# A decode step rebuilt: VectorE's state update replaced by ScalarE products and an adding transfer

## The chip, the cores and the metric

The kernel runs on 1 core of one Trainium2 chip. The metric is device time in microseconds (us): 2167.06 us for the kernel before, the median of 3 runs (2167.03 to 2169.21). Engines are called PE (TensorE), DVE (VectorE), ACT (ScalarE), POOL (GpSimd) and SP (SyncE). Each works through its own instructions in a fixed order and waits on the others by semaphores; SP and POOL also issue the transfers between HBM (the device's memory) and SBUF (the core's memory).

## The reference, cut to what matters

Two layers of a decoder trunk work on 512 prompt tokens and on 8 sample tokens with the same weights. Only the retention of the sample tokens is touched. Per layer, head h (4 of them) and sample b (8 of them) there is a 256 x 256 state S; with one new token the reference comes down to

```python
def retention_chunk(S, q, k, v, log_gamma):      # here L = 1
    scores = einsum('blhd,bmhd->bhlm', q, k) * decay          # decay = 1
    intra = einsum('bhlm,bmhe->blhe', scores, v)              # (q.k) v
    inter = einsum('blhd,bhde->blhe', q, S) * q_dec           # gamma_h (q S)
    S_new = exp(log_gamma * L) * S + einsum('blhd,blhe->bhde', k * k_dec, v)
    return S_new, intra + inter                  # S_new = gamma S + k v,  o = q S_new
```

with gamma_h = 1 - 2^(-5-h). S_new is an output; o goes through a group norm, a gate, and with the other heads into the product with W_out. Everything else of a layer (RMS norm, product with W_in, short convolution, prompt retention, product with W_out, the gate W_pg) is the same in both kernels.

## The kernel before

All tokens stand together as 520 columns. Each of the four big products (W_in's heads, W_in's convolution part, W_out, W_pg) goes through pairs of 128-row output tiles. A pair is done by one level of Strassen's scheme (`strassen`) or directly (`plain`), on fp32 operands split into a high and a low part: three matmuls per weight tile (`mm3`, lines 247 to 249). SP loads weights into a ring of raw tiles (line 312), DVE forms Strassen's sums in place (line 319), ACT writes the high part (line 229) and DVE the low part (line 230) into a second ring, the ring of splits. `SPLIT = 60` blocks of 128 columns are its size; an instruction that fills a part of it has to wait until PE is through with what stood there. Everything else lies in `NSLOT = 75` slots of 520 columns (operands, results, states).

The order on each engine is set at build time by a scheduler, which plans with priorities and with times of its own; `keep(...)` pins an instruction behind the one that was traced before it on its engine. Weight splits have a raised priority.

The decode step is a side line. `head` and the convolution loop call `sample()` about once or twice per pair: some calls lie in the middle of a pair (list `middle`, which `strassen` empties after its fifth product), some at its end. A call first does the step whose operands were loaded by the call before, then issues the next loads. There are 32 steps in a layer, 64 in all; a step is one (h, b):

- `sample_load` (lines 770 and 771): two transfers from POOL's queue: the state (256 KB, transposed so that the 128 partitions hold e, in two halves of 256 columns d) and k, q of this token broadcast to all partitions.
- `sample_step`: ACT scales the state by gamma (line 776), two DVE instructions add k times v (line 780, v is a number per partition in `vs`), POOL issues the store of the new state (line 781), and two DVE instructions form the dot products with q (line 784, result in `osum`).

After the last step of a layer, at the eighth convolution tile (j = 7), `sample_norm` makes the group norm of all 32 results (lines 1371 to 1389, `rsn` on POOL at line 1383) and writes the gated values `gs`. W_out's operands are built from 16 tiles; eight of them are `retained` tiles, each of which takes its last 8 columns from `gs` (line 1064) before it is split (lines 551 and 552). "Joint" below means the stretch from the last convolution pair to the first pairs of W_out.

Of the kernel before, what the change touches and what calls it, by code (L numbers as in the profile page):

```python
# [7 lines left out]
F32 = mybir.dt.float32  # L8
F32R = mybir.dt.float32r
AF = mybir.ActivationFunctionType  # L10
ALU = mybir.AluOpType
MUL, ADD, SUB = ALU.mult, ALU.add, ALU.subtract

P = 128
# [3 lines left out]
SEQ = 512  # L18
NS = 8
T = SEQ + NS  # L20
# [4 lines left out]
H = 4  # L25
# [1 line left out]
PLE = 256  # L27
PAST = 4096
EPS = 1e-6
NSLOT = 75  # L30
CH = 4
CHS = 4
CHA = 4
# [16 lines left out]
EARLY = 6  # L50


HEADS = [[0, 0, 0, 8] + [14] * 12, [0] + [14] * 15]
CONVS = [[14] * 2 + [16] * 13 + [14]] * 2
OUT_ROWS = [[0, 8, 16, 16, 16, 16, 16, 0]] * 2
# [6 lines left out]
RAW = 32  # L62
WARM = 8
FIRST = 8
SPLIT = 60


def F(ap):
# [11 lines left out]
class Slots:  # L80
# [8 lines left out]
    def get(self, dtype=F32):  # L89
        i = self.free.pop(0)  # L90
        self.count += 1
        t = self.pool.tile([P, T], dtype, tag=f"s{i}", name=f"slot{i}_{self.count}")
        self.used[id(t)] = (t, i)
        return t
# [97 lines left out]
def trunk_kernel(  # L192
# [6 lines left out]
    V, S, G, PE, DMA = nc.vector, nc.scalar, nc.gpsimd, nc.tensor, nc.sync  # L199
    SIDE = nc.gpsimd  # L200

    const = ctx.enter_context(tc.tile_pool(name="const", bufs=1))
# [7 lines left out]
    get, getr, put = slots.get, slots.getr, slots.put  # L210
# [6 lines left out]
    keep = tc.keep_in_program_order  # L217
# [340 lines left out]
        return op  # L558


    vec = const.tile([P, 160], F32, name="vec")

    def norm_g(l, k):
        return vec[:, 16 * l + k : 16 * l + k + 1]
# [11 lines left out]
    def kd(h, m):  # L576
        c = 112 + 4 * h + m
        return vec[:, c : c + 1]

    def gam(h):  # L580
        return vec[:, 128 + h : 129 + h]

    ident = const.tile([P, P], F32, name="ident")
    ones = const.tile([P, P], F32, name="ones")
# [4 lines left out]
    vs = const.tile([P, H, 2, NS], F32, name="vs")  # L589
    osum = const.tile([P, 2, H, NS], F32, name="osum")  # L590
# [84 lines left out]
    for a, b in ((0, 1), (1, 4), (4, 8), (8, 12), (12, 16)):  # L675
        raws = []
        if b == 1:
            raw = raw_ring.get(4)
            DMA.dma_start(raw.rearrange("p (m n) -> p m n", n=P), wi[0, 0:4, :, :P].rearrange("m p n -> p m n"))
            S.dma_start(vec, vecs)  # L680
            x = get()
            for n in (LEFT, RIGHT):
                DMA.dma_start(x[:, n], xT[0, :, n])
            xs.append(x)
            w = split_w(raw)
            ws = [[t[:, P * m : P * m + P] for t in w] for m in range(4)]
        else:
            for i in range(4):
                raws.append(load(wi[0, i, :, P * a : P * b]))
                if i < b - a:  # L690
                    x = get()
                    DMA.dma_start(x, xT[a + i])
                    xs.append(x)
            ws = [split_w(raw) for raw in raws]
            raw_ring.put(*raws)
        for k in range(a, b):
            X.ops[k] = split(xs[k], norm_g(0, k), free_src=False, halves=k % 2 == 0 and k < max(X.rows))
            for m in range(4):
                for h, n in enumerate((LEFT, RIGHT)):
                    product(first[m][h], ws[m], k - a, at(X.ops, [k], n), k == 0, k == KT - 1)  # L700
        if b == 1:
            raw_ring.put(raw)
            split_ring.put(*w)
            DMA.dma_start(ident, ident_d)
        else:
            for w in ws:
                split_ring.put(*w)
# [8 lines left out]
    for l in range(DEPTH):  # L716
# [24 lines left out]
        root, rb, rc, rs = prepare()  # L741
# [24 lines left out]
            return g  # L766

        def sample_load(h, b):
            st, kb = get(), get()
            SIDE.dma_start(st[:, :512], sret[l, h, b])  # L770
            SIDE.dma_start(kb[:, :512], kq[l, h, b].rearrange("c d -> (c d)").partition_broadcast(P))  # L771
            return h, b, st, kb

        def sample_step(h, b, st, kb):

            keep(S.activation(st[:, :512], st[:, :512], AF.Identity, scale=gam(h)))  # L776
            k = kb[:, 256:512]
            for e in range(2):
                c = slice(256 * e, 256 * e + 256)
                keep(V.scalar_tensor_tensor(st[:, c], k, vs[:, h, e, b : b + 1], st[:, c], MUL, ADD))  # L780
            SIDE.dma_start(o_rets[l, h, b], st[:, :512])  # L781
            for e in range(2):
                c = slice(256 * e, 256 * e + 256)
                V.tensor_tensor_reduce(k, st[:, c], kb[:, :256], 1.0, 0.0, MUL, ADD, osum[:, e, h, b : b + 1])
            put(st, kb)

        loaded = []

        def sample():

            if loaded:
                sample_step(*loaded.pop(0))
            if todo:
                loaded.append(sample_load(*todo.pop(0)))

        todo = []
# [20 lines left out]
        def retain(h):  # L817
# [28 lines left out]
            vf = []  # L846
            for e, z in enumerate(head(mt + 4)):
                t = z.slot if z.ps is None else copied(z.ps).slot
                V.scalar_tensor_tensor(vs[:, h, e, :], t[:, SEQ:T], 1.0 / 16, rb[:, SEQ:T], MUL, MUL)
                vf.append(t)  # L850
            aside_copy(h, 4, vf)
            todo.extend((h, b) for b in range(NS))
# [224 lines left out]
        for j in range(CJ):  # L1077
# [12 lines left out]
            t = get()  # L1090
# [8 lines left out]
            if j < CJ - 1:  # L1099
                middle.append(sample)  # L1100
            if j == CJ - 1:
                while loaded or todo:
                    sample()
                O.ready = 7
                sample_norm(nc, small, pr, osum, onesd, half_neg, gs, lambda k: gn_g(l, k))
# [45 lines left out]
        for k in range(2):  # L1151
            t = get()
# [326 lines left out]
```

## Time and profile before

| what | value |
|---|---|
| runs | 2169.21, 2167.03, 2167.06 us |
| profiled execution, span from the first to the last instruction | 2167.3 us (the page has no other time for it) |
| mean granted TensorE clock | 0.999 |
| PE busy | 2147.8 us, 17861 matmuls |
| DVE busy | 1896.1 us |
| ACT busy | 1264.5 us |
| POOL busy | 430.6 us |
| DMA, mean over the span | 179 GB/s |

In the profile a row `L780 DVE SCALAR_TENSOR_TENSOR slot<-slot,vs,slot 128x256 ... x128 | 56.1, 481 | 4.5 <-ACT slot L776 4.3` is a group: line, engine, operation, result and operands by the program's names, shape, count; then busy us and mean ns of one; then idle time of the engine just before these instructions and who ended it. The busy us are a union, so that instructions which overlap at their ends give less than count times mean. In a list of waits, `A <- B: total, times, longest` says that A's engine stood idle until B was done. The view of stretches gives the busy time of every engine in each.

### The profile page before, as it was taken

The page shows a single profiled execution, that of the slowest core. Times are in us where ns is not written, and L with a number is a line of the kernel's source. Part 1 is how long each engine was busy: PE and PEld are TensorE (multiplying, and loading weights), DVE is VectorE, ACT ScalarE, POOL GpSimd, SP SyncE. Part 2 cuts the span into 40 slices and gives each one's busy share as a digit, 9 for nine tenths or more (in the row PEclk, how much of TensorE's full clock was granted, in tenths as well). Part 3 has the DMA queues.
Part 4 walks back from the last instruction along what each step waited for, and adds up shares of the span by engine and source line. Part 5 has one row for each costly group of instructions (what it writes and reads, how often), then busy time and mean ns, then how long its engine had stood idle before and what let it go on. Part 6 is the DMA issues. An engine that isn't in the chain of part 4 may idle for free. (4 is left out here: it accounts for less than half of the span.)

```text
span 2167.3 us, 48178 instructions
## 1 busy us (share of the span) xinstructions
PE 2147.8 (99%) x17861; PEld 2142.1 (99%) x17861; DVE 1896.1 (87%) x3849; ACT 1264.5 (58%) x2647; POOL 430.6 (20%) x746
## 2 busy tenths in 40 slices
PE   9999999999999999999999999999999999999998
PEld 9999999999999999999999999999999999999998
DVE  8889988998999987987997988989999998879884
ACT  8656655565555655655765655565645555456565
POOL 2313222211001211200212222231111022011011
PEclk9999999999999999999999999999999999999999
DMA  8555565545543745645645566664464355566455
GB/s 288 171 175 197 181 217 184 178 157 175 158 129 118 238 156 187 215 154 160 215 144 175 172 213 191 189 209 170 151 182 149 120 158 202 176 207 200 128 164 198
DMA packets 182861, 387.31 MB, mean 179 GB/s; under 512 B 25888, under 2 KB 56352, under 8 KB 182624
## 3 DMA queue, kind: packets, MB, share of 16 engines
q1 hardware_dynamic: 128704, 212.98, 31.6%
q0 software_dynamic: 53056, 169.84, 23.8%
q8 instruction: 140, 2.29, 0.4%
q10 hardware_dynamic: 864, 1.39, 0.2%
q14 instruction: 97, 0.79, 0.1%
HBM read 318.96 MB, written 65.15 MB: 177 GB/s over the span
## 5 line engine op out<-in xcount | busy, mean ns | idle before, releaser
L247 PE MATMUL ps_g<-slot,split 128*128 128x260 f32 x5465 | 1531.6, 284 | 7.2 <-ACT slot L307 2.9
L248 PE MATMUL ps_g<-slot,split 128*128 128x260 f32 x5465 | 1534.3, 282 | 0.3 <-DVE slot L555 0.3
L249 PE MATMUL ps_g<-slot,split 128*128 128x260 f32 x5461 | 1519.9, 283 | 0.5 <-DVE split L230 0.5
L229 ACT ACTIVATE split<-raw 128x512 fp32r<-128x512 f32 (+2 forms) x1347 | 777.3, 596 | 583.1 <-DVE raw L319 213.2
L247 PEld LDWEIGHTS ps_g<-slot,split 128*128 128x128 f32 x5465 | 1024.0, 188 | 10.1 <-ACT slot L307 3.7
L248 PEld LDWEIGHTS ps_g<-slot,split 128*128 128x128 f32 x5465 | 1028.5, 188 | 0.5 <-DVE slot L555 0.5
L249 PEld LDWEIGHTS ps_g<-slot,split 128*128 128x128 f32 x5461 | 1019.8, 188 | 1.0 <-DVE split L230 1.0
L230 DVE TENSOR_TENSOR split<-raw,split 128x512 fp32r<-128x512 f32 (+2 forms) x1346 | 849.2, 652 | 172.5 <-PE ps_g L248 85.4
L319 DVE TENSOR_TENSOR raw<-raw 128x512 f32<-128x512 f32 (+1 forms) x660 | 428.9, 660 | 32.5 <-DMA raw<-wi 23.7
L307 ACT ACTIVATE slot<-ps_g 128x260 f32<-128x260 f32 x336 | 127.4, 381 | 140.6 <-PE ps_g L249 122.7
L551 ACT ACTIVATE slot<-slot 128x520 fp32r<-128x520 f32 (+1 forms) x212 | 109.2, 562 | 46.6 <-DVE slot L414 11.1
L552 DVE TENSOR_TENSOR slot<-slot,slot 128x520 fp32r<-128x520 f32 (+1 forms) x212 | 124.4, 620 | 4.1 <-ACT slot L551 3.9
L781 POOL DMA_DIRECT2D o_rets<-slot x64 | 35.3, 552 | 351.6 <-DVE slot L780 131.7
L307 DVE TENSOR_TENSOR slot<-ps_g,slot 128x260 f32<-128x260 f32 x168 | 70.9, 424 | 6.0 <-PE ps_g L249 3.7
L869 POOL DMA_DIRECT2D slot<-hs x64 | 46.2, 724 | 118.7 <-DVE split L230 42.7
L814 POOL DMA_DIRECT2D hs<-slot x64 | 35.6, 556 | 139.3 <-DVE slot L755 61.3
L780 DVE SCALAR_TENSOR_TENSOR slot<-slot,vs,slot 128x256 f32<-128x256 f32 x128 | 56.1, 481 | 4.5 <-ACT slot L776 4.3
L746 DVE TENSOR_TENSOR slot<-slot,slot 128x520 f32<-128x520 f32 x80 | 55.8, 698 | 4.7 <-DMA o_rets<-slot 3.7
L770 POOL DMA_DIRECT2D slot<-sret x64 | 35.5, 554 | 114.6 <-ACT split L229 37.3
L1058 POOL DMA_DIRECT2D slot<-x1s x76 | 40.8, 538 | 87.6 <-PE ps_g L249 27.2
L1209 POOL DMA_DIRECT2D x2s<-slot x30 | 16.4, 545 | 201.6 <-DVE slot L1204 200.6
L771 POOL DMA_DIRECT2D slot<-kq x64 | 34.9, 547 | 106.0 <-DVE slot L876 22.2
(217 smaller groups left out, 1733.8 us busy)
## 6 DMA issues: line engine op xcount, KB each, us to landing
raw<-wi SPq DMA_DIRECT2D x377, 256.0 KB, 3.9
raw<-wo SPq DMA_DIRECT2D x128, 256.0 KB, 5.4
raw<-wg SPq DMA_DIRECT2D x122, 256.0 KB, 4.1
raw<-wi SPq DMA_DIRECT2D x136, 192.0 KB, 4.0
slot<-x1s POOLq DMA_DIRECT2D x76, 260.0 KB, 5.1
slot<-sret POOLq DMA_DIRECT2D x64, 256.0 KB, 4.0
hs<-slot POOLq DMA_DIRECT2D x64, 256.0 KB, 4.0
slot<-hs POOLq DMA_DIRECT2D x64, 256.0 KB, 5.2
```

Source lines behind the costliest of these rows:

```text
L229: S.activation(hi, raw, AF.Copy)
L230: V.tensor_tensor(lo, raw, F(hi), SUB)
L247: PE.matmul(out, wh, xh, start=start, stop=False, skip_group_check=more)
L248: PE.matmul(out, wh, xl, start=False, stop=False, skip_group_check=more)
L249: PE.matmul(out, wl, xh, start=False, stop=stop, skip_group_check=more)
L307: fn(*args)
L319: V.tensor_tensor(out[:, n], x[:, n], y[:, n], op)
L551: keep(S.activation(hi, src[:, n], AF.Copy))
L552: V.tensor_tensor(lo, src[:, n], F(hi), SUB)
L746: V.tensor_tensor(out[:, n], v, table[:, n], MUL)
L780: keep(V.scalar_tensor_tensor(st[:, c], k, vs[:, h, e, b : b + 1], st[:, c], MUL, ADD))
L869: SIDE.dma_start(t[:, :512].rearrange("p (m n) -> p m n", m=2), src)
```

## The change

The decode step is taken apart into three calls instead of two. With S' = S + k v / gamma the new state is gamma S', so v is divided by gamma once (`vs`, line 853 after the change). The load call brings k and q alone. The next call lets ACT write k v / gamma into a fresh slot (two products, line 776 after the change) and has POOL issue a transfer that adds the state from HBM onto that slot (line 777). The call after that does the two dot products on DVE, with gamma as their scale (line 784), then ACT multiplies the slot by gamma (line 785), and POOL stores it (line 786). The dot products and the ACT instructions are pinned with `keep`. DVE's two state updates are gone. One slot more is held while steps are under way (k, q of two steps and one state, before that of one step and its state); `NSLOT` goes to 76, the ring of splits to 56 blocks, and `vec` loses 32 columns.

```diff
-NSLOT = 75
+NSLOT = 76
+GAMMA = [1.0 - 2.0 ** (-5 - h) for h in range(H)]
-SPLIT = 60
+SPLIT = 56
...
         def sample_load(h, b):
-            st, kb = get(), get()
-            SIDE.dma_start(st[:, :512], sret[l, h, b])
+            kb = get()
             SIDE.dma_start(kb[:, :512], kq[l, h, b].rearrange("c d -> (c d)").partition_broadcast(P))
-            return h, b, st, kb
-
-        def sample_step(h, b, st, kb):
-
-            keep(S.activation(st[:, :512], st[:, :512], AF.Identity, scale=gam(h)))
-            k = kb[:, 256:512]
+            return h, b, kb
+
+        def sample_add(h, b, kb):
+
+            st = get()
             for e in range(2):
                 c = slice(256 * e, 256 * e + 256)
-                keep(V.scalar_tensor_tensor(st[:, c], k, vs[:, h, e, b : b + 1], st[:, c], MUL, ADD))
-            SIDE.dma_start(o_rets[l, h, b], st[:, :512])
+                keep(S.activation(st[:, c], kb[:, 256:512], AF.Copy, scale=vs[:, h, e, b : b + 1]))
+            SIDE.dma_start(st[:, :512], sret[l, h, b], accum_op=ADD)
+            return h, b, kb, st
+
+        def sample_step(h, b, kb, st):
+
             for e in range(2):
                 c = slice(256 * e, 256 * e + 256)
-                V.tensor_tensor_reduce(k, st[:, c], kb[:, :256], 1.0, 0.0, MUL, ADD, osum[:, e, h, b : b + 1])
+                keep(V.tensor_tensor_reduce(kb[:, 256:512], st[:, c], kb[:, :256], GAMMA[h], 0.0, MUL, ADD, osum[:, e, h, b : b + 1]))
+            keep(S.activation(st[:, :512], st[:, :512], AF.Copy, scale=GAMMA[h]))
+            SIDE.dma_start(o_rets[l, h, b], st[:, :512])
             put(st, kb)
 
-        loaded = []
+        loaded, added = [], []
 
         def sample():
 
+            if added:
+                sample_step(*added.pop(0))
             if loaded:
-                sample_step(*loaded.pop(0))
+                added.append(sample_add(*loaded.pop(0)))
             if todo:
                 loaded.append(sample_load(*todo.pop(0)))
...
-                V.scalar_tensor_tensor(vs[:, h, e, :], t[:, SEQ:T], 1.0 / 16, rb[:, SEQ:T], MUL, MUL)
+                V.scalar_tensor_tensor(vs[:, h, e, :], t[:, SEQ:T], 1.0 / 16 / GAMMA[h], rb[:, SEQ:T], MUL, MUL)
...
-                while loaded or todo:
+                while added or loaded or todo:
```

The scheduler places everything anew, so that thousands of rows stand elsewhere. Three places show what the steps below rest on. The first is POOL in the head stage of layer 1, around the fifth decode step (its state is `slot_200_2382` before, `slot_199_2374` after). Before:

```order
L770 DMA slot_200_2382<-sret 128x512
L869 DMA slot_206_2526<-hs 128x2x256
L869 DMA slot_217_2960<-hs 128x2x256
L771 DMA slot_201_2383<-kq 128x512
L781 DMA o_rets<-slot_183_2055 128x512
L770 DMA slot_207_2560<-sret 128x512
L781 DMA o_rets<-slot_200_2382 128x512
```

With the change:

```order
L768 DMA slot_200_2378<-kq 128x512
L786 DMA o_rets<-slot_182_2047 128x512
L777 DMA slot_199_2374<-sret 128x512
L786 DMA o_rets<-slot_199_2374 128x512
L777 DMA slot_206_2552<-sret 128x512
L768 DMA slot_207_2556<-kq 128x512
```

Before, the state's load (L770) is issued ahead of the store of an earlier step and of other loads. Now the adding load (L777) stands right behind the store of the step before it (L786), and the store of its own state right behind it.

The second place is DVE at the same step: from the second dot product of the step before (result in `osum`, state `slot_182_2047`) to the first one of this step (state `slot_199_2374`). With the change:

```order
L784 ISA slot_174_1906,osum<-slot_182_2047,slot_174_1906 128x256
L784 ISA osum 128x1
L231 TENSOR_TENSOR split<-raw,split 128x512
L231 TENSOR_TENSOR split<-raw,split 128x256 x2
L231 TENSOR_TENSOR split<-raw,split 128x384
L922 SCALAR_TENSOR_TENSOR slot_204_2515<-ps_vt,r5p,slot_203_2514 128x256
L320 TENSOR_TENSOR raw<-raw 128x384
L231 TENSOR_TENSOR split<-raw,split 128x512
L320 TENSOR_TENSOR raw<-raw 128x384
L922 SCALAR_TENSOR_TENSOR slot_204_2515<-ps_vt,r5p,slot_203_2514 128x256
L320 TENSOR_TENSOR raw<-raw 128x512
L784 ISA slot_183_2051,osum<-slot_199_2374,slot_183_2051 128x256
```

Between them lie ten instructions of other work (the row with x2 is two); between them in time the state has to go through ACT's scaling, ACT's products, POOL's two issues and the adding transfer.

The third place is DVE at the joint of layer 1: the last two operations of `sample_norm` (`dl<-dl,rsn` and `gs<-dl,vec,gs`). Before:

```order
L230 TENSOR_TENSOR split<-raw,split 128x512
L1385 TENSOR_TENSOR dl<-dl,rsn 128x32 x2
L1108 TENSOR_TENSOR slot_445_8698<-slot_445_8698,slot_448_8929 128x520
L319 TENSOR_TENSOR raw<-raw 128x512
L1389 SCALAR_TENSOR_TENSOR gs<-dl,vec,gs 128x8 x2
L230 TENSOR_TENSOR split<-raw,split 128x512 x2
L1389 SCALAR_TENSOR_TENSOR gs<-dl,vec,gs 128x8 x6
L746 TENSOR_TENSOR slot_445_8698<-slot_447_8709,slot_445_8698 128x520
```

With the change:

```order
L553 TENSOR_TENSOR slot_469_9263<-slot_461_9183,slot_469_9263 128x260
L1393 SCALAR_TENSOR_TENSOR gs<-dl,vec,gs 128x8 x5
L1097 SCALAR_TENSOR_TENSOR slot_464_9192<-slot_463_9187,vec,slot_464_9192 128x510
L1099 SCALAR_TENSOR_TENSOR slot_464_9192<-scv,vec,slot_464_9192 128x8
L1393 SCALAR_TENSOR_TENSOR gs<-dl,vec,gs 128x8
L308 TENSOR_TENSOR slot_466_9229<-ps_g,slot_466_9229 128x260
L1393 SCALAR_TENSOR_TENSOR gs<-dl,vec,gs 128x8 x2
L553 TENSOR_TENSOR slot_470_9264<-slot_461_9183,slot_470_9264 128x260
```

Before, `gs` is finished at the gating of the seventh convolution tile (L1108 and L746 on `slot_445_8698`). Now, since the last step ends one call later, it is finished during the convolution of the eighth (L1097) and among the splits of W_out's operands (L553 is line 552 of before).

More of the change, by code (lines that the diff above doesn't have):

```diff
@@ L558, in split @@
         return op
-    vec = const.tile([P, 160], F32, name="vec")
+    vec = const.tile([P, P], F32, name="vec")
     def norm_g(l, k):
@@ L578, in kd @@
         return vec[:, c : c + 1]
-    def gam(h):
-        return vec[:, 128 + h : 129 + h]
     ident = const.tile([P, P], F32, name="ident")
@@ L679, in trunk_kernel @@
             DMA.dma_start(raw.rearrange("p (m n) -> p m n", n=P), wi[0, 0:4, :, :P].rearrange("m p n -> p m n"))
-            S.dma_start(vec, vecs)
+            S.dma_start(vec, vecs[:, :P])
             x = get()
```

## The prediction

> **What bounds the kernel now.** I read the page's head first, then the view of stretches cut at the stages (start, layer 1's heads, its convolution, the joint, W_out and W_pg, then layer 2 alike), then PE's waits.
>
> ```profile
> span 2167.3 us, 48178 instructions
> PE 2147.8 (99%) x17861; PEld 2142.1 (99%) x17861; DVE 1896.1 (87%) x3849; ACT 1264.5 (58%) x2647; POOL 430.6 (20%) x746
> ```
> ```profile
> 0.00:70.00 70.00, 67.24 (x527) 65.85 (x528) 56.12 (x111) 53.32 (x103) 18.41 (x40) 1.00 0.73 246
> 70.00:390.00 320.00, 320.00 (x2677) 320.00 (x2677) 290.18 (x638) 192.01 (x423) 90.41 (x157) 1.00 0.60 191
> 390.00:700.00 310.00, 309.06 (x2581) 308.81 (x2580) 281.55 (x565) 169.96 (x346) 43.97 (x66) 1.00 0.49 152
> 700.00:730.00 30.00, 26.68 (x218) 26.07 (x218) 30.00 (x65) 24.88 (x68) 10.58 (x20) 1.00 0.81 272
> 730.00:1100.00 370.00, 370.00 (x3090) 369.98 (x3089) 317.39 (x602) 219.14 (x425) 62.34 (x117) 1.00 0.58 184
> 1100.00:1440.00 340.00, 339.39 (x2832) 338.41 (x2831) 299.11 (x655) 196.31 (x437) 87.40 (x146) 1.00 0.58 181
> 1440.00:1770.00 330.00, 329.12 (x2743) 328.08 (x2742) 303.28 (x615) 184.11 (x380) 49.24 (x75) 1.00 0.50 154
> 1770.00:1800.00 30.00, 28.15 (x233) 27.72 (x232) 29.66 (x65) 23.10 (x64) 10.14 (x19) 1.00 0.83 287
> 1800.00:2090.00 290.00, 290.00 (x2417) 289.99 (x2417) 245.12 (x446) 158.35 (x301) 45.17 (x85) 1.00 0.54 174
> 2090.00:2167.30 77.30, 68.17 (x564) 67.22 (x562) 43.73 (x96) 43.35 (x105) 12.99 (x23) 0.98 0.55 187
> ```
>
> A row is a stretch, its length, then the busy time of PE, PEld, DVE, ACT, POOL, the granted clock, DMA share and GB/s. PE is the bound: it idles 19.5 us in all. By stage: 2.8 at the start, 2.4 in the four stretches that hold decode steps (0 + 0.94 + 0.61 + 0.88), 5.2 in the two joints (3.32 + 1.85), nothing in W_out and W_pg, 9.1 at the end. A matmul takes 2147.8 / 17861 = 0.120 us of PE, and the change leaves their number. So whatever DVE gains, the decode stages can return 2.4 us, 0.11% of the time. In the joints DVE is the busy one (30.00 of 30, 29.66 of 30).
>
> ```profile
> PE ps_g L247 <- ACT split L229: 1.3, 1, 1.3
> PE ps_g L247 <- ACT ps_g L307: 1.2, 1, 1.2
> PE ps_vt L913 <- DMA slot<-hs: 0.9, 1, 0.9
> PE ps_st L248 <- DVE slot L918: 0.5, 1, 0.5
> DVE split L230 <- PE ps_g L248: 85.4, 109, 2.2
> ACT split L229 <- PE ps_g L249: 186.2, 220, 3.9
> ```
>
> The first two are waits in joint 1, the next two are decode-stage waits, the last two are over the whole span: DVE and ACT often wait for PE to free a part of the ring of splits. They run ahead by up to the whole ring: 60 blocks are 30 weight tiles in two parts, three matmuls each, 30 x 3 x 0.120 = 10.8 us; with 56 blocks 28 x 0.36 = 10.1 us. That is the cover under which DVE may stand still unseen.
>
> **The change part by part.**
>
> ```profile
> L780 DVE SCALAR_TENSOR_TENSOR slot<-slot,vs,slot 128x256 f32<-128x256 f32 x128 | 56.1, 481 | 4.5 <-ACT slot L776 4.3
> L784 DVE CUSTOM_DVE_ANT_0 slot<-slot,slot 128x256 f32<-128x256 f32 x128 | 53.9, 421 | 0.0
> L776 ACT ACTIVATE slot<-slot,vec 128x512 f32<-128x512 f32 x64 | 45.7, 714 | 0.0
> L1281 ACT ACTIVATE slot<-slot,vec 128x256 f32<-128x256 f32 x14 | 7.0, 497 | 2.4 <-DMA slot<-x2s 2.4
> L874 ACT ACTIVATE slot<-slot 128x512 fp32r<-128x512 f32 x48 | 28.7, 624 | 10.1 <-DMA yc<-slot 4.6 <-DVE slot L904 2.4 <-DVE osum L784 2.1
> L781 POOL DMA_DIRECT2D o_rets<-slot x64 | 35.3, 552 | 351.6 <-DVE slot L780 131.7 <-issue 81.3 <-ACT split L229 72.7
> ```
>
> DVE loses 128 state updates, 56.1 us; its dot products stay. ACT loses 64 x 0.714 and gains per step two products of 256 columns with a number per partition (nearest row L1281, 0.497) and one scaling of 512 (L874, 0.624): 64 x (0.994 + 0.624 - 0.714) = +57.9 us. That takes ACT from 58% to 61%, with each decode stretch under 66%; it lies beside PE, under the same ring. If that cover were gone, a close step would cost 0.9 us. POOL issues three transfers per step as before. Path cost of these edits: nothing. The gain on PE is between 0 and the 2.4 us of the decode stages; its waits there are one late transfer and late split or product rows, some of which a lighter DVE removes. I take half: -1.2.
>
> The new wait is the dot product's for the adding transfer. No row shows such a transfer. Lower bound: a plain load of the state. Upper bound: that load and then a store of the same size, one after the other.
>
> ```profile
> slot<-sret POOLq DMA_DIRECT2D x64, 256.0 KB, 4.0
> o_rets<-slot POOLq DMA_DIRECT2D x64, 256.0 KB, 3.1
> DMA to landing us min/median/max: 2.8/4.0/7.3
> DMA to landing us min/median/max: 2.2/3.1/7.2
> L780 DVE SCALAR_TENSOR_TENSOR slot<-slot,vs,slot x4: 480/481/484, 280.5 to 289.6; 128x256 f32<-128x256 f32 x4
> L780 DVE SCALAR_TENSOR_TENSOR slot<-slot,vs,slot x38: 477/482/493, 102.3 to 385.6; 128x256 f32<-128x256 f32 x38
> L230 DVE TENSOR_TENSOR split<-raw,split 128x512 fp32r<-128x512 f32 x1031 | 695.0, 690 | 147.8 <-PE ps_g L248 81.2 <-ACT split L229 51.8 <-issue 6.1
> L230 DVE TENSOR_TENSOR split<-raw,split 128x256 fp32r<-128x256 f32 x66 | 27.3, 423 | 8.5 <-ACT split L229 7.6 <-PE ps_g L248 0.8
> ```
>
> So 4.0 to 7.1 us (medians). In the head stage 19 steps stand in 283 us, but unevenly: a call in a pair's middle and the one at its end follow each other closely (8.7 us in the row 280.5 to 289.6). By the starts of L780, 9 of the 18 gaps of layer 1's heads are under 13 us. In such a gap DVE has, by the order shown, ten instructions of 0.42 to 0.69 us between the two dot products, about 5.5 us. Meanwhile the chain runs: ACT's scaling 0.62, its products 0.99, POOL's store issue 0.55, the adding transfer 4.0 to 7.1: 6.2 to 9.3 us. The dot product comes 0.7 to 3.8 us too early, and DVE, in order, stands that long with the splits queued behind it; ACT's scaling behind it waits too. I take the middle, 2.2 us. 18 such steps are 13 to 68 us of DVE standing still, 6 to 34 in 320 us of heads, where the lost updates free 38 x 0.44 = 16.7 and 29.8 are idle now. Both single wait and sum fit under the cover of 10.1 us, so PE pays nothing: cost 0, at worst some tenths per step where DVE is behind already.
>
> [...]
>
> The ring of splits: 10.1 us instead of 10.8 us of cover; the W_out and W_pg stretches have no PE idle at all, so 0.7 us less should stay unseen: 0, and up to +2 in the joints. One slot more is eaten by the steps, and free afterwards: 0.
>
> What is moved is the last step's end. A step now ends one call later; in the convolution the calls are some 20 us apart:
>
> ```profile
> L780 DVE SCALAR_TENSOR_TENSOR slot<-slot,vs,slot x4: 479/480/483, 1706.6 to 1726.9; 128x256 f32<-128x256 f32 x4
> L1389 DVE SCALAR_TENSOR_TENSOR gs<-dl,vec,gs x8: 222/222/225, 683.7 to 685.9; 128x8 f32<-128x8 f32 x8
> L1064 ACT ACTIVATE slot<-gs x12: 192/198/211, 710.1 to 729.3; 128x8 f32<-128x8 f32 x12
> L1389 DVE SCALAR_TENSOR_TENSOR gs<-dl,vec,gs x8: 222/224/227, 1753.5 to 1755.7; 128x8 f32<-128x8 f32 x8
> L1064 ACT ACTIVATE slot<-gs x12: 193/198/208, 1777.0 to 1798.2; 128x8 f32<-128x8 f32 x12
> ```
>
> `gs` now has 24.2 us (685.9 to 710.1) and 21.3 us (1755.7 to 1777.0) before its first reader. Less 20.3 (or 18 to 20 elsewhere) it keeps about 4 and 1 us. It isn't late yet, but its eight products (8 x 0.22 = 1.8 us) now fall into the joint, where DVE has no idle time and PE waits already. Cost between 0 and 1.8 per joint; I take 0.6 each, +1.2.
>
> Sum: 2167.3 - 1.2 + 1.2 = 2167.3 for the profiled execution; it stands 0.2 above the median of the runs, so 2167.
>
> **The rivals.**
>
> - *Joints gain too.* The joints' 5.2 us come from late ACT copies and splits; a reshuffled order, one free slot more and DVE's earlier finish could remove them. With the decode stages: at most 2167.3 - 2.4 - 5.2 = 2159.7; by half of it and more, about 2161.5. For it: these waits are few (single ones of 1.2 and 1.3 us). Against: in the joints nothing of DVE's work is removed.
> - *`gs` comes late* (slower). If the adding transfer or the pinned dot products push the last step by more than the 4 and 1 us left, each further us is one of PE's, since `retained` tiles feed the first pair of W_out. From 4 us on it decides; 3 to 5 us per joint give 2173 to 2177, say 2174.
> - *The adding transfer is slow* (slower). At the longest rows, 7.3 + 7.2 = 14.5 us, a close step's wait is 16.7 - 5.5 = 11.2, more than the cover; half the cover is used up by other bursts, so from a transfer of about 8.3 us on PE pays. At 10 us: 18 x (6.7 - 5) = 30, thus 2197. Against: the longest rows are rare.
>
> **How the numbers follow.** No change 0.52, at 2167, its own range 2162.7 to 2171.4 (0.2% each way, about what a measurement of this kernel can tell from no change); joints gain 0.20; `gs` late 0.16; slow transfer 0.12. So faster 0.20, same 0.52, slower 0.28. The range takes in nearly all of the first two and half of the third: 2160 to 2176.
>
> **What would show it.** Right: DVE busy near 1840 us, ACT near 1322; L776's products near 0.50 us; the dot products wait for `slot<-sret`, in total 13 to 68 us, most of it in the head stages; PE idle in 70 to 700 and 1100 to 1770 below 2.4 us; landing of the adding transfer between 4 and 7.1. Wrong: PE waiting for splits in the heads (slow transfer), PE idle above 5 us in a joint with L1064's reader last (`gs` late), or PE's 0.120 us per matmul moved, for which I have no reason.

## The result, and the profile after

The changed kernel takes 2190.6 us (median of 4 runs, 2185.7 to 2191.0), the kernel before 2167.5: the ratio is 1.0102, with a 95% interval of 1.0087 to 1.0116. It is slower by about 22 us, where 2167 was predicted. The profiled execution is the fastest of the four (2185.7, span 2183.9), 16.6 us above the span of before; the traces are compared over these 16.6.

The page's first part, busy time by engine:

```profile
span 2183.9 us, 48474 instructions
PE 2155.9 (99%) x17861; PEld 2147.8 (98%) x17861; DVE 1856.0 (85%) x3721; ACT 1303.4 (60%) x2775; POOL 455.9 (21%) x746
```

DVE is 40 us lighter, ACT 39 heavier. PE's matmuls are as many as before, but busy for 8.1 us longer, and PE idles 28.0 us instead of 19.5: half of the 16.6 us is waiting, and half is a longer busy time for the same matmuls. The view of stretches for the changed kernel, cut at the same matmuls as the stages of before (heads 1, convolution 1, joint 1, W_out and W_pg 1, then layer 2 alike; columns as in the prediction):

```profile
70.50:395.70 325.20, 322.97 (x2679) 322.10 (x2678) 276.77 (x598) 202.74 (x462) 98.34 (x158) 0.99 0.63 187
395.70:707.00 311.30, 309.67 (x2583) 309.46 (x2582) 275.23 (x536) 180.28 (x374) 46.71 (x72) 1.00 0.53 156
707.00:735.20 28.20, 26.58 (x220) 26.28 (x219) 28.00 (x68) 21.17 (x57) 11.70 (x14) 1.00 0.68 234
735.20:1107.40 372.20, 370.92 (x3092) 370.50 (x3091) 318.42 (x608) 220.66 (x434) 63.98 (x119) 1.00 0.57 185
1107.40:1452.60 345.20, 341.95 (x2835) 339.52 (x2834) 288.95 (x625) 206.09 (x474) 95.65 (x145) 1.00 0.60 179
1452.60:1784.70 332.10, 330.09 (x2745) 329.88 (x2744) 293.36 (x571) 195.18 (x408) 53.05 (x80) 0.99 0.52 155
1784.70:1816.50 31.80, 30.06 (x236) 29.72 (x235) 31.80 (x77) 24.21 (x64) 10.93 (x15) 0.95 0.71 230
1816.50:2107.80 291.30, 290.50 (x2420) 290.23 (x2419) 244.56 (x444) 158.13 (x301) 46.79 (x87) 1.00 0.54 175
```

Cut at the same matmuls, these stages lasted 320.2, 310.4, 30.2, 370.2, 340.4, 330.3, 30.3 and 290.2 us before. So the two head stages lose 5.0 and 4.8 us, the convolutions 0.9 and 1.8, joints with W_out and W_pg 2.6 together, start and end 1.5. The loss sits where the decode steps stand closest. What PE, DVE and ACT wait for there (the list of waits over the span: total, times, longest):

```profile
PE ps_g L248 <- ACT slot L308: 7.7, 6, 2.0
PE ps_g L248 <- ACT split L230: 2.7, 4, 1.4
PE ps_g L248 <- ACT ps_g L308: 2.5, 3, 1.6
DVE slot L784 <- DMA slot<-sret: 27.5, 14, 3.3
ACT slot L785 <- DVE osum L784: 47.5, 34, 3.2
ACT slot L308 <- DMA o_rets<-slot: 18.2, 9, 3.4
DVE slot L744 <- DMA o_rets<-slot: 7.2, 2, 4.9
```

In this list, PE's first and third rows are its waits for L308 (L307 of before), ACT's copy of a finished product out of PSUM: 10.2 us now, 4.5 before (2.9 and 1.6). Only 3.3 of the 10.2 us lie in the two head stages. The next four rows are the decode step's new waits: dot products (L784) for the adding transfer, ACT's scaling (L785) for the dot products, and other instructions for a slot whose state is still being stored. One stall shows how they meet. The waits between 1469 and 1480 us, around PE's longest stall:

```profile
ACT slot L763 <- DVE slot L744: 5.7, 1, 5.7
DVE slot L744 <- DMA o_rets<-slot: 4.9, 1, 4.9
PE ps_g L248 <- ACT slot L308: 2.0, 1, 2.0
```

A store of a state was issued at 1467.5 and landed at 1475.9. DVE's L744 takes the stored slot and stands 4.9 us for it; ACT's L763 waits for L744, and the copy L308, which PE needs to go on, is queued on ACT behind L763. That ACT and DVE are many splits ahead of PE doesn't help: the copy can't be made early.

Of the other half, more than half is the clock. The stretch behind PE's stall at 345.8 us, and one behind a shorter stall at 413.4:

```profile
349.00:352.50 3.50, 3.50 (x19) 3.50 (x18) 2.49 (x5) 1.54 (x4) 2.41 (x5) 0.52 0.86 323
352.50:356.00 3.50, 3.50 (x31) 3.50 (x31) 3.50 (x10) 2.27 (x5) 0.00 (x0) 0.99 0.02 5
413.00:417.00 4.00, 2.37 (x20) 2.16 (x19) 4.00 (x13) 3.36 (x10) 0.44 (x1) 1.00 0.74 241
```

PE is busy throughout in the first row, yet does 19 matmuls instead of the 31 of the row after it: the granted clock was 0.52. The changed kernel has three such stretches of 3.41 us at half clock (349.1, 1478.9 and 1810.0 us), behind stalls of 2.0 to 2.3 us, counted from one matmul's start to the next, and each holds 15 to 16 matmuls of 0.216 us, 1.5 us lost; before had none but at its end. Together that is some 4.6 of the 8.1 us; the rest of the longer busy time was not followed.

### The profile page after: what moved, and what is told of

Its sections match the earlier page's. It is cut to its first block, busy times and chain, and to the rows that moved or that the text cites. A ratio compares the mean times of both kernels' runs of the same rounds, so it can differ in the third digit from the quotient of the medians.

```text
span 2183.9 us, 48474 instructions
## 1 busy us (share of the span) xinstructions
PE 2155.9 (99%) x17861; PEld 2147.8 (98%) x17861; DVE 1856.0 (85%) x3721; ACT 1303.4 (60%) x2775; POOL 455.9 (21%) x746
## 3 DMA queue, kind: packets, MB, share of 16 engines
q8 instruction: 140, 2.29, 0.4%
## 5 line engine op out<-in xcount | busy, mean ns | idle before, releaser
L308 ACT ACTIVATE slot<-ps_g 128x260 f32<-128x260 f32 x336 | 124.2, 372 | 49.1 <-PE ps_g L250 24.6
L786 POOL DMA_DIRECT2D o_rets<-slot x64 | 35.7, 558 | 454.7 <-ACT slot L785 437.9
L553 DVE TENSOR_TENSOR slot<-slot,slot 128x520 fp32r<-128x520 f32 (+1 forms) x212 | 121.9, 609 | 2.5 <-ACT slot L552 2.1
L308 DVE TENSOR_TENSOR slot<-ps_g,slot 128x260 f32<-128x260 f32 x168 | 70.9, 422 | 8.5 <-PE ps_g L250 7.1
L784 DVE CUSTOM_DVE_ANT_0 slot<-slot,slot 128x256 f32<-128x256 f32 x128 | 53.5, 418 | 27.7 <-DMA slot<-sret 27.5
L785 ACT ACTIVATE slot<-slot 128x512 f32<-128x512 f32 x64 | 40.2, 629 | 49.3 <-DVE osum L784 47.5
L777 POOL DMA_DIRECT2D slot<-sret x64 | 56.6, 884 | 40.0 <-ACT slot L308 18.5
L744 DVE TENSOR_TENSOR slot<-slot,slot 128x520 f32<-128x520 f32 x80 | 55.3, 691 | 7.2 <-DMA o_rets<-slot 7.2
```

Of the source, the lines that this page charges most:

```text
L308: fn(*args)
L553: V.tensor_tensor(lo, src[:, n], F(hi), SUB)
L744: V.tensor_tensor(out[:, n], v, table[:, n], MUL)
L777: SIDE.dma_start(st[:, :512], sret[l, h, b], accum_op=ADD)
L784: keep(V.tensor_tensor_reduce(kb[:, 256:512], st[:, c], kb[:, :256], GAMMA[h], 0.0, MUL, ADD, osum[:, e, h, b : b + 1]))
```

## The experiments

Times are medians; a ratio is to the kernel before, timed in the same batch, with its 95% interval. "Waits for the transfer" is the row `DVE slot L784 <- DMA slot<-sret` of each run. The changed kernel has 76 slots and 56 blocks in its ring of splits; since its step holds one slot more, it has as many slots free as the kernel before with 75.

The theories: the *adding transfer* (it lands late), the *late store* (a slot is taken while its state is still being stored), the *ring* (56 blocks are too few) and the *reshuffled order* (the scheduler places everything anew; later also "chosen order", that of before being a lucky one). From the fifth kernel on also the *queue* (waits of the decode step on DVE and ACT hold up copies out of PSUM queued behind them) and the *late last step* (`gs`).

**A plain load for the adding transfer** (every engine's order as in the changed kernel):

```diff
-            SIDE.dma_start(st[:, :512], sret[l, h, b], accum_op=ADD)
+            SIDE.dma_start(st[:, :512], sret[l, h, b])
```

> The changed kernel, but the transfer of the state doesn't add: it overwrites the product k v, so that the new state lacks that term. Every engine's order of instructions is the same as in the changed kernel, so only the transfer differs. Theory 'adding transfer' (its second read and its packets make it and its neighbours land late): landing of the state's load falls from 4.4 to about 4.0 us, the issue on GpSimd from 884 to about 550 ns, waits of others for the stores fall from 28 us to under 20, and at least 8 of the 23 us come back: 2182 or less. Theory 'late store' (a step's store is now its last act and goes out behind ACT's scaling, and the slot it reads is the one that a copy out of PSUM takes next): the stores leave at the same places, the waits for them stay near 28 us, the time stays at 2187 to 2191. Theory 'ring' and theory 'reshuffled order': 2187 to 2191 too.

Measured: 2180.5 us, 1.0061 [1.0044, 1.0078], 10.2 us less than the changed kernel. The view of the state's tensor tells the landing, of the changed kernel and of this one:

```profile
DMA to landing us min/median/max: 3.7/4.4/9.1
```
```profile
DMA to landing us min/median/max: 2.8/3.4/7.6
```

The groups by line tell the issue on POOL, of the changed kernel and of this one:

```profile
L777 POOL DMA_DIRECT2D slot<-sret x64 | 56.6, 884 | 40.0 <-ACT slot L308 18.5 <-ACT slot L776 15.4 <-ACT split L230 3.5
```
```profile
L777 POOL DMA_DIRECT2D slot<-sret x64 | 34.8, 543 | 40.3 <-ACT slot L308 18.1 <-ACT slot L776 16.1 <-ACT slot L921 2.8
```

The add costs 1.0 us of landing and 0.3 us of POOL per transfer; the waits for the transfer fall from 27.5 to 16.2 us, while those of DVE and ACT for stores fall only from 28 to 24. The gain of the profiled execution (5.2 us) sits in the two head stages, where the waits are: 321.5 and 343.8 us here, 325.2 and 345.2 in the changed kernel.

```profile
70.40:391.90 321.50, 320.99 (x2679) 320.38 (x2678) 277.37 (x598) 204.44 (x462) 91.80 (x158) 1.00 0.60 190
1104.80:1448.60 343.80, 341.07 (x2836) 339.31 (x2835) 291.73 (x629) 209.14 (x478) 86.42 (x146) 1.00 0.57 180
```

So the add is worth about 10 of the 22 us (by the two ratios 9, and by their intervals 4 to 14). Its later landing and its longer issue on POOL (22 us over the 64 transfers) change together here and aren't told apart. How it reaches PE isn't seen either: PE's waits for copies are 10.2 us over the span in this run too.

```profile
PE ps_g L248 <- ACT slot L308: 5.2, 5, 2.2
PE ps_g L248 <- ACT ps_g L308: 5.0, 4, 2.0
```

**One slot more**, `NSLOT = 77`:

> The changed kernel with 77 slots instead of 76, ring of splits as it is (56). Slots go round in order, so each is taken up one turn later. Theory 'late store': waits of ACT and DVE for stores of the state fall from 28 us to under 20, the two stalls of PE over 2 us that end in such a wait (345.8 and 1476.2 us) go, with the stretches of slow matmuls behind them (1.5 us each): 5 to 9 us less, 2182 to 2186. Theory 'ring': nothing, 2189 to 2192. Theory 'reshuffled order': anything from 2184 to 2197, with stalls at new places.

Measured: 2194.8 us, 1.0121 [1.0104, 1.0138]. ACT and DVE wait 19 us for stores (28 before the edit) and 20.0 us for the transfer, and the time is no better.

**The slot of k and q goes back first**, `put(kb, st)`:

> The changed kernel with put(kb, st) for put(st, kb): the slot of k and q goes back ahead of the state's, which is so taken up one turn later; nothing else. Theory 'late store': as with 77 slots, 3 to 9 us less, 2182 to 2188. Theories 'ring' and 'adding transfer': 2189 to 2192. Theory 'reshuffled order': 2184 to 2197.

Measured: 2199.9 us, 1.0148 [1.0131, 1.0164]: 9 us slower; 25.4 us of waits for the transfer. In this run's trace two of PE's four stalls over 2 us and three shorter ones lead back, by the instructions queued ahead of a copy, to a dot product that stood 1.6 to 4.6 us for its adding transfer. Followed back in the same way (at each step to the wait that ended last), none of the 15 stalls of over 0.14 us that PE has in the changed kernel itself, between 70 and 2124 us, ends at a dot product's wait for the adding transfer. Three of them, 4.1 us together, end at a late store (at 345.8, 1263.8 and 1476.2 us), the others at other transfers, at the ring or at no wait within 15 us. With the half clock behind the first and the last of the three, late stores so account for 7 of the 16.6 us. Yet two edits that should have cured the late store gained nothing, so that it isn't confirmed as the main cause.

**The ring at 60 blocks again**, `SPLIT = 60`, with the 76 slots:

> The changed kernel with its ring of splits at 60 blocks again, 76 slots as they are. Theory 'ring': the stall of 1.91 us at 413.4 us (a copy queued on ACT behind a split that waited 4.5 us for room in the ring) goes, and others; at least 8 us come back, 2182 or less. Theory 'late store': 0 to 3 us less, 2187 to 2191, the waits for stores near 28 us. Theory 'reshuffled order': 2184 to 2197.

Measured: 2190.8 us, 1.0108 [1.0092, 1.0123]: nothing came back. With the new step the four blocks aren't what is missing; with the old step they are, as later runs show.

**The new step for half the heads, the old one for the others** (`h < 2` new, and `h >= 2` new):

```diff
+            if h < 2:          # second kernel: h >= 2
                 kb = get()
...
+            st, kb = get(), get()
+            ...                # load and step as before the change
```

> The new step for heads 0 and 1 of each layer (16 of 32 steps, all in the head stage, some 9 to 20 us apart), the old step for heads 2 and 3 (3 in the head stage, 13 in the convolution, 20 us apart); 76 slots, ring 56 as in the changed kernel. Theory 'queue' (a dot product that waits for the adding transfer, or a slot that waits for a late store, holds up DVE and with it ACT, and behind them in order the copies out of PSUM that PE needs at once; this hurts where steps follow closely): nearly the whole loss stays, 2181 to 2192. Theory 'traffic' (the adding transfer itself, in every step alike): about half of the loss, 2176 to 2181. Theory 'late last step' (the group norm a call later): no loss, under 2172, since the last step is an old one here.

> The other half: the old step for heads 0 and 1, the new step for heads 2 and 3 (13 of these 16 in the convolution). Theory 'queue': nearly no loss, 2166 to 2174. Theory 'traffic': about half, 2176 to 2181. Theory 'late last step' or 'slots and ring' (76 and 56 are kept): the whole loss, 2186 to 2192.

Measured: 2204.0 us, 1.0165 [1.015, 1.018], and 2193.2 us, 1.011 [1.0095, 1.0126]. Neither half is free of loss. They can't be read further: where the old step runs, one slot more is free, and that alone moves the time by as much (below).

**A call more between the adding transfer and the dot products** (78 slots, and 52 blocks):

```diff
-            if added:
+            if len(added) > 1 or added and not loaded and not todo:
                 sample_step(*added.pop(0))
```

> The changed kernel with one call more between the adding transfer and the dot products (two adding transfers under way); 78 slots for it, and a ring of splits of 52 blocks, since no more fits. Theory 'queue', if the wait for the adding transfer is its cause: the waits of the dot products fall from 27.5 us to under 5, most of the loss comes back, 2168 to 2178. If the late stores' slots are: waits for stores stay near 28 us, 2182 to 2192. Theory 'traffic': 2184 to 2192. Theory 'ring' (52 blocks): slower than the changed kernel, 2193 or more.

Measured: 2202.4 us, 1.0162 [1.0145, 1.0179]. The dot products wait for the transfer no more, but ACT, POOL and DVE wait 38 us for stores, and the ring is down to 52 blocks, whose price was not measured. So the waits for the transfer are gone and no time came back, against the theory 'queue' (2168 to 2178) and as the theory 'ring' expected (2193 or more); by the change in the ring it doesn't decide.

**Sizes alone, on the kernel before** (old step): `SPLIT = 56`; `SPLIT = 64`; `NSLOT = 76`; both `SPLIT = 56` and `NSLOT = 76`; and, as a small reshuffle, `put(kb, st)`:

> The kernel before with a ring of 56 blocks, nothing else. Theory 'ring': a good part of the loss, 2176 or more. Theories 'queue' and 'traffic': 2164 to 2171. Theory 'reshuffled order' (any edit makes the scheduler place everything anew, and the kernel before stands at a lucky order): 2172 to 2190 although no mechanism asks for it.

> The kernel before with a larger ring of splits, 64 blocks. Theory 'ring' (56 blocks are too few; the kernel before lost 23 us with them): more cover can't hurt, 2160 to 2170. Theory 'chosen order' (the order that the scheduler made of the kernel before is by chance, or by choice among many, a good one, and any edit that moves thousands of rows falls back to an ordinary order some 20 us worse): 2178 to 2200.

> The kernel before with 76 slots, ring 60: only more room. Theory 'ring' and theory 'queue': 2160 to 2170. Theory 'chosen order': 2178 to 2200.

> The kernel before with put(kb, st) for put(st, kb), the twin of the same edit on the changed kernel, which cost 9 us there. It moves a quarter as many rows on TensorE as the ring's edits. Theory 'queue' and 'ring': 2164 to 2171. Theory 'chosen order': slower here too, 2171 to 2195.

> The kernel before with the sizes of the changed kernel, 76 slots and a ring of 56, and the old decode step: what is left between this and the changed kernel is the decode step alone. Theory 'chosen order': 2180 to 2200, so that the new step by itself costs between -10 and +10. Theory 'queue': 2166 to 2176, and the new step costs 15 to 25.

Measured: 56 blocks 2191.4 us, 1.0101 [1.0084, 1.0117]; 64 blocks 2168.4, 0.9992 [0.9981, 1.0003]; 76 slots 2186.4, 1.0077 [1.0062, 1.0092]; `put(kb, st)` 2167.9, 0.9997 [0.9987, 1.0006]; both sizes 2205.2, 1.017 [1.0155, 1.0185]. Four things follow. A thoroughly reshuffled order need not be slower (with 64 blocks 6108 of the 17861 matmuls stand elsewhere by their line and operands, and it costs nothing): the theory of a lucky order falls in its general form. The smaller ring alone costs the old step 23 us, as much as the whole change. A free slot more costs 17: the operands of later pairs are built ahead as far as the number of free slots allows (`fill` compares `len(slots.free)` with a reserve), so `NSLOT` sets the order of the work and not only its room; how that costs PE wasn't followed. And the old step at the changed kernel's own sizes, 76 slots and 56 blocks, is 14.6 us slower than the new one, which neither theory expected (between -10 and +10 us for the new step, or 15 to 25 us of cost); with 56 blocks and as many slots free (75) the two steps take the same, 2191.4 and 2190.6 us.

What the ring costs is seen in the kernel before with 56 blocks, its view of stretches (joint 2; W_out and W_pg 1; heads 2) and its waits:

```profile
731.20:1105.30 374.10, 371.99 (x3092) 371.79 (x3092) 317.15 (x604) 221.81 (x429) 63.52 (x117) 1.00 0.57 183
1105.30:1450.60 345.30, 340.11 (x2834) 338.58 (x2833) 301.14 (x657) 196.78 (x441) 87.28 (x148) 1.00 0.57 181
1780.90:1817.70 36.80, 31.96 (x236) 30.83 (x235) 34.42 (x74) 25.48 (x68) 9.59 (x18) 0.91 0.73 240
```
```profile
PE ps_g L247 <- ACT split L229: 10.0, 9, 2.7
PE ps_g L247 <- ACT slot L307: 2.5, 5, 0.7
```

PE waits for splits more than for copies, and the loss is in the joint (36.8 us against 30.3), in W_out and W_pg (374.1 against 370.2) and in heads 2 (345.3 against 340.4). The first two are other places than the new step's; but heads 2 is one of the two stages in which the changed kernel loses most, and the ring alone loses as much there with the old step, without an adding transfer.

**The ring at 58 blocks on the kernel before**, and with 60 blocks the new step with a plain load, with dot products that aren't pinned, and with the next state's products ahead of the step:

```diff
-                keep(V.tensor_tensor_reduce(..., GAMMA[h], 0.0, MUL, ADD, osum[...]))
+                V.tensor_tensor_reduce(..., GAMMA[h], 0.0, MUL, ADD, osum[...])
```
```diff
-            if added:
-                sample_step(*added.pop(0))
             if loaded:
                 added.append(sample_add(*loaded.pop(0)))
+                if len(added) > 1:
+                    sample_step(*added.pop(0))
+            elif added:
+                sample_step(*added.pop(0))
```

> The kernel before with a ring of 58 blocks (60: 2168, 64: 2168, 56: 2191). Theory 'ring as cover': between the two, 2172 to 2184. Theory 'order' (each size gives another order, good or bad by chance): either 2164 to 2171 or 2184 to 2200, nothing between.

> The new step with the ring at 60 blocks (2190.8 us) and a plain load for the adding transfer, so that the new state lacks k v; every engine's order is that of the run with 60 blocks. Theory 'adding transfer' (its later landing and its packets): 8 to 14 us less, as at 56 blocks, 2177 to 2183, with the dot products' waits down from 31 us to about 20. Theory 'order': 2188 to 2194.

> The new step with the ring at 60 blocks and the dot products free of their pin, so that the scheduler may put them elsewhere on VectorE. Theory 'queue' (a dot product that stands for the adding transfer, and copies out of PSUM behind it): the waits for the adding transfer fall below 15 us, 2175 to 2185. Theory 'adding transfer': 2186 to 2194. Theory 'order': 2184 to 2200.

> The new step with the ring at 60 blocks, each call first forming the next state's products and issuing its adding transfer, then doing the step whose transfer was issued a call ago. The adding transfer so leaves ahead of the store and isn't behind ACT's scaling, 2 to 4 us earlier. Theory 'queue': the dot products' waits fall from 31 us to under 10, 2172 to 2183. Theory 'late store' (slots held by stores): 2188 to 2196, waits for stores 26 us or more. Theory 'order': 2184 to 2200.

Measured: 58 blocks 2183.8 us, 1.006 [1.0042, 1.0078], between 60 and 56 and at the edge of both theories' ranges: with the old step the price grows, in these three sizes, with what is taken from the ring. Plain load 2178.4, 1.0042 [1.0027, 1.0057], 12.4 us less than its twin of the same order; again the profiled executions' whole gain (6.6 us) lies in the two head stages. Unpinned 2243.0, 1.0345 [1.0309, 1.0381]. Products first 2187.2, 1.0078 [1.006, 1.0096]. The waits of these three and of their parent with 60 blocks (in the order parent, plain, unpinned, products first):

```profile
DVE slot L784 <- DMA slot<-sret: 31.1, 13, 3.8
```
```profile
DVE slot L784 <- DMA slot<-sret: 16.0, 10, 2.6
```
```profile
DVE slot L784 <- DMA slot<-sret: 119.9, 54, 5.6
PE ps_g L248 <- ACT slot L308: 19.0, 13, 2.7
PE ps_g L248 <- DVE slot L308: 15.2, 14, 1.8
PE ps_g L248 <- ACT ps_g L308: 12.4, 7, 3.3
```
```profile
DVE slot L784 <- DMA slot<-sret: 30.1, 10, 4.4
```

Without the pin the scheduler sets the dot products too early: DVE stands 54 times, 120 us in all, and PE waits 46.6 us for copies out of PSUM on ACT and DVE; the first head stage takes 338.3 us, 14.5 more than in the parent, though no single wait is longer than 5.6 us and the ring would cover that. Here the waits are seen to go through to PE: followed back, 35 of its stalls of over 0.14 us, 38.0 us together, lead to a dot product that stood for its transfer; in the parent six do, 5.9 us. The run was slower than every theory expected. Products first shortens ACT's wait for the dot products (28.8 to 13.8 us) but not the waits for the transfer, and gains 3.6 us.

**Calls spaced evenly in the head stage**, with 60 blocks on the new step and on the kernel before:

```diff
             if m // 2 % 2:
                 middle.append(sample)
+            else:
+                early_calls.append(sample)     # strassen empties it after its second product
...
-            sample()
+            if not m // 2 % 2:
+                sample()
```

> The new step with the ring at 60 blocks, and the calls of the head stage spaced evenly: of two pairs the first has its call after the fifth product as now and none at its end, the second gets one after its second product beside the one at its end, so that calls stand some 13 us apart instead of 8, 20 and 13. Nothing else. Theory 'queue': the dot products' waits for the adding transfer fall from 31 us to under 10, and at 0.5 to 0.6 us of TensorE per us of waiting 10 to 14 us come back: 2175 to 2182. Theory 'adding transfer' (its traffic, not the wait): 2186 to 2194. Theory 'order': 2180 to 2200 with waits that don't tell it.

> The kernel before (old step, ring 60, 75 slots) with the same even calls. Its dot products wait for no transfer, so theory 'queue': 2164 to 2174, and the new step then costs 5 to 12 us instead of 22. Theory 'order' (a call moved is enough to lose the good order): 2178 to 2195.

Measured: 2206.0 us, 1.0166 [1.0146, 1.0187], and 2187.5 us, 1.0091 [1.0076, 1.0106]. The cure didn't take: the waits grew to 43.0 us (L789 is L784 here), and the calls cost the old step 20 us by themselves. The difference between the two steps stays at 18.5 us.

```profile
DVE slot L789 <- DMA slot<-sret: 43.0, 20, 4.3
```

**Put together.** The five kernels with the new step and 60 blocks, by their waits for the transfer, are 16.0, 30.1, 31.1, 43.0 and 119.9 us against 2178.4, 2187.2, 2190.8, 2206.0 and 2243.0: from the first to the last 0.62 us of time for each us of waiting, and back to no waits at all about 2168, the time of before. Only the pair 16.0 and 31.1 has one order; in the others more was moved than the waits, and the unpinned run largely sets the slope, so that this line is a sign and no measurement of one thing. The new step's other kernels don't lie on it: with 56 blocks 2180.5 us at 16.2 us of waits (plain load), 2194.8 at 20.0 (77 slots), 2199.9 at 25.4 (`put(kb, st)`) and 2190.6 at 27.5, and with 52 blocks 2202.4 without such waits.

By the times that were expected, 'adding transfer' was met by both runs with a plain load. 'Queue' named a time for eleven runs and was met by one (`put(kb, st)` on the kernel before), 'order' for fifteen and was met by five. Of the seven edits of the kernel before, two cost nothing and five 14 to 36 us, so that what the scheduler's order is worth by itself isn't excluded as the rest of the loss; no run keeps the order of before with the new step.

The two causes don't add: new step alone (60 blocks) +22, ring alone (old step) +23, both +23. By stage, against before: heads and convolutions lose 12.5 us with the new step and 56 blocks, 16.2 with it and 60, and 4.8 with the old step and 56. Joints, W_out and W_pg lose 12.0 us with the old step and 56 blocks, but 2.6 with the new step and 56 and 4.5 with it and 60. Why these stages bear a small ring better with the new step wasn't tried, nor was the new step run with more than 60 blocks. No version beat the kernel before.

## Why the prediction was wrong

*PE is the bound, and DVE's gain can return 2.4 us at most.* Right, and nothing of it came: PE idles 9.1 us in the four stages that hold decode steps (2.2, 1.6, 3.3 and 2.0), where less than 2.4 was the mark.

*Costs of the parts.* Products 0.496 us and scaling 0.629 us, as taken. DVE 1856 instead of 1840, ACT 1303 instead of 1322: the busy times are unions, and overlaps changed.

```profile
L776 ACT ACTIVATE slot<-slot,vs 128x256 f32<-128x256 f32 x128 | 57.6, 496 | 5.1 <-DMA ys<-slot 5.1
L785 ACT ACTIVATE slot<-slot 128x512 f32<-128x512 f32 x64 | 40.2, 629 | 49.3 <-DVE osum L784 47.5 <-issue 1.1 <-ACT slot L308 0.7
```

*The new wait: a transfer of 4.0 to 7.1 us, 13 to 68 us of standing still.* Right in size: 4.4 us in the median, 27.5 us in 14 waits (15.4 us in layer 1 and 12.1 in layer 2), all but 1.9 us in the head stages. That such a transfer is harmless, as the sum had it, did not hold.

*"Both single wait and sum fit under the cover of 10.1 us, so PE pays nothing: cost 0."* **This is the step that failed.** A plain load in the adding transfer's place, with every engine's order the same, takes 11 and 15 us of these waits away and returns 10 and 12 us (at 56 and 60 blocks), in the traces all of it in the head stages. So the add cost about half of the loss, where the sum had 0. The flaw in the argument is what the ring covers: splits. The copies out of PSUM stand on the same two engines, in order, and each can start only when its product is done, so that splits made ahead don't help a copy that stands behind a wait. That a wait reaches PE in this way is seen in the unpinned run, where 89 us more of waiting cost 52 us. In the changed kernel itself it is seen for late stores alone (4.1 us, and 3.0 us of half clock behind two of them): in its head stages PE waits 3.3 us for copies, while the dot products wait 25.6 us for the transfer, so that most single waits did stay covered. By which way the add's cost comes to PE there stays open, and so does the other half of the loss. "One slot more ... free afterwards: 0" left out that the store became the step's last act; the three stalls behind late stores stand against that 0, but as a main cause it was not confirmed.

*"10.1 us instead of 10.8 us of cover ... 0, and up to +2 in the joints."* The second term that failed: alone, on the old step, some 14 us for two blocks less and 23 for four. The argument "no PE idle in W_out and W_pg, so 0.7 us less should stay unseen" took a stage without idle time for one with a margin; that stage went from 370.2 to 374.1 us. In the changed kernel itself the term isn't visible, since 60 blocks give nothing back. The same holds the other way round: at 56 blocks and as many slots free, the old step is as slow as the new one. So the runs don't divide the 23 us between step and ring.

*`gs` comes late.* It came later than forecast, with 0.1 and 0.5 us left where 4 and 1 us were expected, and no cost of it is seen: the last of its products ends at 724.9, the first reader starts at 725.0; 1799.1 and 1799.6 in layer 2. No instruction waited for it; joint 1 is shorter than before (28.2 us against 30.2), joint 2 longer (31.8 against 30.3), with a stretch of half clock in it (granted clock 0.95 over the joint). The rows of `gs`'s last operation and of its reader, layer 1, then layer 2:

```profile
L1393 DVE SCALAR_TENSOR_TENSOR gs<-dl,vec,gs x8: 213/216/218, 722.6 to 724.7; 128x8 f32<-128x8 f32 x8
L1068 ACT ACTIVATE slot<-gs x14: 190/193/200, 725.0 to 750.2; 128x8 f32<-128x8 f32 x14
...
L1393 DVE SCALAR_TENSOR_TENSOR gs<-dl,vec,gs x8: 212/213/213, 1798.0 to 1798.9; 128x8 f32<-128x8 f32 x8
L1068 ACT ACTIVATE slot<-gs x14: 191/193/193, 1799.6 to 1825.4; 128x8 f32<-128x8 f32 x14
```

*The rivals.* "Joints gain" and "`gs` late" did not happen. "The adding transfer is slow" was nearest: it named the place (close steps in the heads) and the direction, but set the point from which PE pays at 8.3 us of landing, by half the ring's cover; the add cost 10 us at a median landing of 4.4.

*"PE's 0.120 us per matmul moved, for which I have no reason."* It moved to 2155.9 / 17861 = 0.1207; 4.6 of the 8.1 us behind it are the half clock after stalls of 2.0 to 2.3 us, the rest was not followed.

## What to carry to other kernels

Cover is counted per consumer, not per engine: an engine that runs ten microseconds ahead with one kind of work (splits) can still be just in time with another (copies out of PSUM). A new wait for a transfer, put in order ahead of the second kind, can reach the bound engine; in the unpinned run more than half of it did. So where a transfer is to be waited for on such an engine, look at what is queued behind it and price the wait, even if it fits under the cover; here the add in the transfer cost 10 us where 0 was summed. That more room between the issue and its reader pays was not shown: the run with a call more had no such waits and was slower, with a smaller ring. Sizes that were tuned (a ring, a number of slots by which work is built ahead) are part of the order of work: price each one alone, and compare two versions of a step at equal sizes too, since four blocks of the ring cost the old step as much as the whole change.

## What the runs showed of the hardware

The granted clock fell to half behind three stalls of PE. In the trace of the changed kernel six gaps between the starts of two matmuls are longer than 1.7 us. Behind those of 2.06, 2.29 and 2.02 us (from 345.8, 1476.2 and 1806.7 us) the clock stood at half for 3.41 us, from 349.1, 1478.9 and 1810.0 us on; behind those of 1.91, 1.90 and 1.72 us (from 413.4, 730.1 and 1335.6 us) it stayed full. In the trace of the kernel before the longest gap is 1.58 us, and the clock stays full up to 2164.2 us, after the last matmul. What decides whether the clock falls was not shown.

An adding transfer of 256 KB took 4.4 us to land (median) against 3.4 for a plain one at the same place in the same order, and 884 ns of POOL for its issue against 543.
